# A wait for a gate transfer moved behind the first level's decays, and three weight casts moved behind the copies of v's second tile

## The chip, the core and the metric

The kernel runs on one core of one Trainium2 chip. A core has five engines with instruction streams of their own: PE (TensorE, matrix products; its weight loads are shown as PEld), DVE (VectorE), ACT (ScalarE), POOL (GpSimd) and SP, whose queue here issues nearly all DMA transfers. DVE, ACT, POOL and SP each work through their stream in the order in which the program lists it, so an instruction that waits holds up whatever stands behind it. The metric is the device time of one execution in microseconds (us), as the median of several runs.

## The reference

One inference step of one decoder layer over 1024 prompt tokens and eight short sample sequences of 8 tokens (1088 tokens together), in float32. One projection `w_in` (1024 x 7168) feeds two groups of recurrent heads; their outputs go through `w_out` and a residual.

```python
xn = rmsnorm(x, g_norm); proj = xn @ w_in            # xm zm om | fh qh ih zh
xc = silu(causal_conv(xm)); q, k = xc_h @ w_q, xc_h @ w_k; v = xm_h @ w_v
gates = concat(q, k, v) @ w_gate + b_gate             # ig, log_sigmoid -> lf
hm = mlstm_scan(q, k, v, ig, lf, C0, n0, m0)          # 4 heads, running-max stabiliser m
oh = hgrn2_scan(silu(qh), (1-lb)*sigmoid(-fh), ih, log(lb+(1-lb)*sigmoid(fh)), S0)   # 8 heads
y = x + concat(gated layernorm(hm), gated rmsnorm(oh)) @ w_out; y = rmsnorm(y, g_final)
```

The stabiliser `m` of the mLSTM heads is a running recurrence over the tokens, m_t = max(lf_t + m_(t-1), ig_t), started anew at each sample's first token from a given state.

## The kernel before, in words

**Exact float32 products.** Every large product is made of three passes: both operands are split into a high part and the remainder (`whi`, `wlo` for a block of weights, `XH`, `XL` for the tokens), and `mm3` issues high x high, low x high and high x low into one PSUM buffer (lines L94 to L96). A weight block of 128 output columns is loaded into `wraw`, cast to `whi` on ACT, and `wlo` is the difference, made on POOL or DVE (all three in `w_split`, line L147). `whi` and `wlo` have two buffers each, `wraw` three.

**The front.** `front_conv` makes two blocks of `xm` for each mLSTM head through `in_block`, whose token columns come in three chunks of 384, 384 and 320 (24 matmuls each). Each chunk lands in one of three PSUM buffers named `mm` and is emptied by ACT (L477 into `xmh`, L478 into `XB`) and DVE (L479 into `xml`). The third chunk also holds the samples' columns: L481 and L482 on ACT, L483 on DVE. `convolve` follows on DVE (L503, then L506 three times). `front_v` multiplies `xm` by `w_v` in nine tiles of 128 tokens, six matmuls each; each tile takes one of the three `mm` buffers and is emptied by two ACT copies, L540 (256 columns of v) and L541 (8 gate columns, into `GTOK` for head 0 and `GST` for the others). I number the tiles t0 to t8.

**Which block is split when.** In a call of `in_block` with one block, `blk_split(nxt)` splits the next block's weights ahead of the chunks. Blocks 5, 7 and 9 are split in the calls that follow `front_v` of heads 1, 2 and 3 in the program.

**The gate scans.** After the front, `gate_scan` writes the gates of all heads and tokens to memory (`gd`, L595), reads them back in rows of one head each (L597, four transfers: `glf`, `gt`, `ig`, `gy`), and runs two scans on DVE. In the scan of `m` the samples' first tokens are cut off by writing -1e30 into eight columns of `t1` (the tile `gt`), line L604. The scan itself is L606; `lm` (L603) is the start of the samples, and it had been put behind `ctxs["k2"]`, the copy of the first level's decays into `Sf` (L1038).

**The heads.** `hgrn_main` works a head in levels. For the first level DVE and ACT make `Q1`, `K1` (L1022, L1023, L987) from `hq` and `hk`, and PE then runs 72 small matmuls in a burst (L101). PE's order is written by `weave`, which slips the next blocks' `in_block` matmuls between the pieces of a head.

**What sets the order.** Up to the fourth `xm` block, the orders of PE, ACT, DVE and POOL are as written. Then a scheduler that works with a model of time places the instructions of all engines (from the heads on, PE's order is again as written), within the data's own order; `behind(i, r)` adds to it that `i` may not come before `r` on their engine.

Of the kernel before, what the change touches and what calls it, by code (L numbers as in the profile page):

```python
# [17 lines left out]
T = 1088  # L18
TP = 1024
# [11 lines left out]
def hybrid_step(  # L31
# [8 lines left out]
    V, S, G, PE = nc.vector, nc.scalar, nc.gpsimd, nc.tensor  # L40
# [28 lines left out]
    def ps_mm():  # L69
        return pm.tile([P, 512], F32, tag="mm", name=nm("mm"))  # L70
# [21 lines left out]
    def mm3(out, lhs, rhs, first, last):  # L92
        (lh, ll), (rh, rl) = lhs, rhs
        PE.matmul(out, lhsT=lh, rhs=rh, start=first, stop=False)  # L94
        PE.matmul(out, lhsT=lh, rhs=rl, start=False, stop=False)  # L95
        PE.matmul(out, lhsT=ll, rhs=rh, start=False, stop=last)  # L96
# [22 lines left out]
    r = 0  # L119
# [22 lines left out]
    def w_split(key, eng=G):  # L142
        raw = wq[key]
        hi = wp.tile([P, 1024], F32R, tag="whi", name=nm("whi"))
        lo = wp.tile([P, 1024], F32R, tag="wlo", name=nm("wlo"))
        wq[key] = (hi.rearrange("p (k c) -> p k c", c=P), lo.rearrange("p (k c) -> p k c", c=P))
        return S.copy(hi, raw), eng.tensor_tensor(lo, raw, f32(hi), op=ALU.subtract)  # L147
# [16 lines left out]
    def blk_load(i):  # L164
        if i < len(blocks) and ("w", i) not in wq:
            kind, j = blocks[i]
            o = boff[kind] + j * P
            return w_load(("w", i), w_in[0, :, o:o + P].rearrange("(k p) c -> p k c", p=P))

    def blk_split(i, eng=None):  # L170
        if i < len(blocks) and not isinstance(wq[("w", i)], tuple):
            return w_split(("w", i), eng or (V if i in v_splits else G))
# [34 lines left out]
    def xchunk(X, c):  # L207
        t0, n = CH[c]
        return X[:, 8 * t0:8 * t0 + 8 * n].rearrange("p (k c) -> p k c", c=n)
# [41 lines left out]
    def in_block(*items):  # L251


        ws = []
        for kind, j, evac in items:
            i = bidx[(kind, j)]
            if i > 1 or len(items) == 1:
                if ("w", i) in wq and not isinstance(wq[("w", i)], tuple):
                    blk_split(i)
            ws.append(i)  # L260
        for i in ws:
            blk_load(i + 2)
        nxt = ws[-1] + 1
        if len(items) == 1:
            blk_split(nxt)
        for c, (t0, n) in enumerate(CH):
            xh, xl = xchunk(XH, c), xchunk(XL, c)
            for (kind, j, evac), i in zip(items, ws):
                wh, wl = wq[("w", i)]
                ps = ps_mm()  # L270
                for k in range(8):
                    mm3(ps[:, :n], (wh[:, k, :], wl[:, k, :]), (xh[:, k, :], xl[:, k, :]), k == 0, k == 7)
                    if k % 2 and k < 7:
                        yield cost(6, n)
                evac(c, t0, n, ps)
                yield cost(6, n)
# [8 lines left out]
    ctxs = {}  # L285
# [93 lines left out]
    def behind(i, r):  # L379

        if r is None:
            return
        tc.add_manual_dep(getattr(i, "ins", i), getattr(r, "ins", r).name, mybir.DependencyInfo(
            mybir.DependencyClass.NoSync, mybir.DependencyReason.DATA), reason="behind")
# [42 lines left out]
    GTOK = cp.tile([P, 9, 8], F32, name="GTOK")  # L427
    GST = cp.tile([P, 9, 8], F32, name="GST")
# [96 lines left out]
    def front_v(h):  # L525
        wh, wl = qkv_w[h]
        xms = [fr[2 * h + a]["m"] for a in range(2)]
        for t in range(9):
            ps = ps_mm()
            u = t % 2  # L530
            if u == 0:
                vt = half("vt")
                vv = vt[:, :2 * VW].rearrange("p (a c) -> p a c", c=VW)
                G.memset(vv[:, :, 256:257], 1.0)
                G.memset(vv[:, :, 257:258], 0.0)
            for a in range(2):
                o = 512 + a * 264
                mm3(ps[:, :264], (xms[a][0][:, t * P:(t + 1) * P], xms[a][1][:, t * P:(t + 1) * P]),
                    (wh[:, o:o + 264], wl[:, o:o + 264]), a == 0, a == 1)
            S.copy(vv[:, u, 0:256], ps[:, :256])  # L540
            S.copy((GST if h else GTOK)[:, t, :], ps[:, 256:264])  # L541
            if t == 8:
                nc.sync.dma_start(out=vsd[h], in_=vt[:, :VW])
            elif u:
                nc.sync.dma_start(out=vd[h, :, (t - 1) * VW:(t + 1) * VW], in_=vt[:, :2 * VW])
            yield

        if h:
            V.tensor_tensor(GTOK, GTOK, GST, op=ALU.add)
# [33 lines left out]
    def gate_scan():  # L583

        ig, y, lf, t1, m, b = [unit(s)[0:4, :T] for s in ("ig", "gy", "glf", "gt", "gm", "gb")]

        lg = half("lg")
        LF = lg[:, 0:272]
        V.tensor_scalar(GT, GT, scalar1=bgt, scalar2=None, op0=ALU.add)
        S.activation(LF, GT, AF.Abs)  # L590
        S.activation(LF, LF, AF.Exp, scale=-1.0)
        S.activation(LF, LF, AF.Ln, bias=1.0)
        V.scalar_tensor_tensor(LF, GT, 0.0, LF, op0=ALU.min, op1=ALU.subtract)
        for i, src in enumerate((GT, LF)):
            nc.sync.dma_start(out=gd[i], in_=src)  # L595
        for i, dst in ((1, lf), (1, t1), (0, ig), (0, y)):
            nc.sync.dma_start(out=dst.rearrange("p (j t) -> p j t", t=272),  # L597
                              in_=gd[i].rearrange("(j r) t -> r j t", r=32)[4 * i:4 * i + 4])
        yield 1.0
        lfs = lf[:, TP:T].rearrange("p (b c) -> p b c", c=8)[:, :, 0]  # L600
        igs = ig[:, TP:T].rearrange("p (b c) -> p b c", c=8)[:, :, 0]
        lm = small(8, "lm")
        behind(V.tensor_tensor(lm[0:4, :], lfs, m0t, op=ALU.add), ctxs["k2"])  # L603
        V.memset(t1[:, TP:T].rearrange("p (b c) -> p b c", c=8)[:, :, 0], -1e30)  # L604
        V.tensor_tensor(y[:, TP:T].rearrange("p (b c) -> p b c", c=8)[:, :, 0], igs, lm[0:4, :], op=ALU.max)
        V.tensor_tensor_scan(m, t1, y, initial=0.0, op0=ALU.add, op1=ALU.max)  # L606
        yield 4.0
        G.memset(t1, 1.0)
        G.memset(t1[:, 0:TP].rearrange("p (b c) -> p b c", c=P)[:, :, 0], 0.0)
        G.memset(t1[:, TP:T].rearrange("p (b c) -> p b c", c=8)[:, :, 0], 0.0)  # L610
        st = lf[:, 0:TP].rearrange("p (b c) -> p b c", c=P)[:, 1:8, 0]
        V.tensor_tensor(st, st, m[:, 0:TP].rearrange("p (b c) -> p b c", c=P)[:, 0:7, 127], op=ALU.add)
        V.tensor_copy(lfs, lm[0:4, :])
        V.tensor_tensor_scan(b, t1, lf, initial=0.0, op0=ALU.mult, op1=ALU.add)
        V.tensor_tensor(y, b, m, op=ALU.subtract)
        nc.sync.dma_start(out=rd, in_=y)
        V.tensor_tensor(ig, ig, b, op=ALU.subtract)
        nc.sync.dma_start(out=o_pm[0, 0].unsqueeze(1), in_=m[:, TP - 1:TP])
        msl = small(8, "msl")
        V.tensor_copy(msl[0:4, :], m[:, TP:T].rearrange("p (b c) -> p b c", c=8)[:, :, 7])  # L620
        nc.sync.dma_start(out=o_sm[0].rearrange("b h -> h b"), in_=msl[0:4, :])
        yield 6.5
        ps = ps_o()
        for t in range(8):
            PE.transpose(ps[:, t * 8:t * 8 + 4], ig[:, t * P:t * P + P], ident[0:4, 0:4])
            PE.transpose(ps[:, t * 8 + 4:t * 8 + 8], m[:, t * P:t * P + P], ident[0:4, 0:4])
        for j in range(4):
            for o, src in ((64, ig), (68, m)):
                PE.matmul(ps[32 * j:32 * j + 32, o:o + 4], lhsT=src[:, TP + win(j):TP + win(j) + 32],
                          rhs=ident[0:4, 0:4], start=True, stop=True)  # L630
        V.tensor_copy(COLS.rearrange("p a b -> p (a b)"), ps[:, :72])
        S.activation(COLS[:, :, 4:8], COLS[:, :, 4:8], AF.Exp, scale=-2.0)
        yield 0.5

        co = unit("co")
        for kk in range(2):
            pt = ps_o()
            for k in range(4):
                PE.transpose(pt[:27, k * P:(k + 1) * P], CS[:, kk * 4 + k, :], ident)
            V.tensor_copy(co[:27, kk * 512:(kk + 1) * 512], pt[:27, :])  # L640
        nc.sync.dma_start(out=o_pconv[0, 0], in_=co[0:3, :DM])
        nc.sync.dma_start(out=o_sconv[0].rearrange("b j d -> (b j) d"), in_=co[3:27, :DM])
        yield 0.5
# [1078 lines left out]
```

## Time and profile before

| | |
|---|---|
| time, median of 3 runs | 1149.5 us (1148.18 to 1153.0) |
| time of the profiled execution | 1149.5 us |
| span of the profiled execution | 1147.7 us, so 1.8 us lie around it |
| mean granted TensorE clock | 0.995 |
| PE busy | 1123.9 us, 98% of the span |
| DVE, ACT, POOL busy | 749.7, 471.1, 239.7 us |
| DMA | 133.53 MB, mean 116 GB/s |

Times in the profile are in us from the span's start unless marked ns. A row of the timeline has start, duration, engine, line, operation, what is written and read, sizes, a count, and in brackets the idle time of the engine ahead of it and what ended it. A row of the waits has the engine, tile and line that waited, what it waited for, the total, the number of times and the longest. Matmuls overlap, so one of 0.33 us can start 0.17 us after another: the pace is read from the starts.

### The profile page before, as it was taken

Reading aid. Unit: us, or ns where it says so; the run is one execution under the profiler, and the core shown is the slowest. Engines: PE = TensorE matmul, PEld = TensorE weight load, DVE = VectorE, ACT = ScalarE, POOL = GpSimd, SP = SyncE. Lnnn points to the kernel's source line nnn. Section 1 sums busy time; section 2 is a strip of 40 time slices with the busy share of each in tenths; the row PEclk is TensorE's granted clock in tenths of the full one; section 3 lists DMA queues with packets and bytes.
Section 4 is the critical chain, followed back from the end, with each engine's and each line's share of the span. In section 5 each row is a group of like instructions: output and inputs, shape, how many; then the busy total and the mean of one; then the engine's idle time right before and its main releaser. Section 6 shows DMA issues by size and latency. Waiting matters only on the chain.

```text
span 1147.7 us, 22956 instructions
## 1 busy us (share of the span) xinstructions
PE 1123.9 (98%) x9255; PEld 1056.0 (92%) x9255; DVE 749.7 (65%) x1484; ACT 471.1 (41%) x1047; POOL 239.7 (21%) x396
## 2 busy tenths in 40 slices
PE   7989999899999999999999999999999999999997
PEld 6889999899999999999999999999999998888886
DVE  6656454494778567784779567877677687545533
ACT  6455455335432553235423453252524344243332
POOL 3204333002530144203530153102020200100000
PEclk9999999999999999999999999999999999999999
DMA  7243342222324242334124331422221255567662
GB/s 225 85 150 123 113 157 101 86 56 94 104 83 152 60 152 78 119 95 136 56 78 153 117 112 60 134 77 78 57 78 57 68 171 159 153 196 208 191 191 91
DMA packets 154154, 133.53 MB, mean 116 GB/s; under 512 B 11500, under 2 KB 130376, under 8 KB 154048
## 3 DMA queue, kind: packets, MB, share of 16 engines
q1 hardware_dynamic: 154046, 132.06, 36.9%
q8 instruction: 73, 1.20, 0.4%
q14 instruction: 33, 0.27, 0.1%
q10 hardware_dynamic: 2, 0.00, 0.0%
HBM read 93.47 MB, written 38.57 MB: 115 GB/s over the span
## 4 chain that ended last, share of the span: by engine, by line
PE 88%; DVE 5%; ACT 3%; DMA 2%; issue 2%; POOL 0%; SPq 0%; POOLq 0%; DVEq 0%; ACTq 0%
PE mm L94 24%; PE mm L95 23%; PE mm L96 23%; PE lv L101 2%; PE o L1216 1%; PE o L1235 1%; PE o L94 1%; PE o L95 1%; PE o L96 1%; PE o L1238 1%; DMA mraw<-mixd 1%; PE lv L1197 1%; PE o L1130 1%; PE mm L1338 1%; PE mm L1340 1%
## 5 line engine op out<-in xcount | busy, mean ns | idle before, releaser
L94 PE MATMUL mm<-XH,whi 128*128 128x384 f32 (+1 forms) x1344 | 450.4, 335 | 0.0
L95 PE MATMUL mm<-XL,whi 128*128 128x384 f32 (+1 forms) x1344 | 439.4, 327 | 0.4 <-DVE XL L245 0.4
L96 PE MATMUL mm<-XH,wlo 128*128 128x384 f32 (+1 forms) x1344 | 439.2, 327 | 0.0
L94 PEld LDWEIGHTS mm<-XH,whi 128*128 128x128 f32 x1344 | 253.5, 189 | 3.1 <-issue 2.5
L95 PEld LDWEIGHTS mm<-XL,whi 128*128 128x128 f32 x1344 | 253.5, 189 | 1.8 <-issue 0.9
L96 PEld LDWEIGHTS mm<-XH,wlo 128*128 128x128 f32 x1344 | 252.9, 188 | 0.0
L147 ACT CAST whi<-wraw 128x1024 fp32r<-128x1024 f32 x54 | 56.7, 1051 | 87.2 <-PE mm L95 67.2
L147 POOL TENSOR_TENSOR wlo<-wraw,whi 128x1024 fp32r<-128x1024 f32 x30 | 71.8, 2392 | 84.3 <-ACT whi L147 84.0
L1328 ACT CAST mhi<-mraw 128x1024 fp32r<-128x1024 f32 (+1 forms) x32 | 31.9, 998 | 69.3 <-PE mm L95 50.5
L974 POOL MEMSET A<- 128x288 f32 x8 | 2.7, 342 | 261.8 <-ACT A L1103 261.8
L94 PE MATMUL mm<-XH,mhi 128*128 128x512 f32 x144 | 56.8, 395 | 0.0
L96 PE MATMUL mm<-XH,mlo 128*128 128x512 f32 x144 | 56.3, 391 | 0.2 <-DVE mlo L1329 0.2
L95 PE MATMUL mm<-XL,mhi 128*128 128x512 f32 x144 | 56.1, 389 | 0.0
L1329 DVE TENSOR_TENSOR mlo<-mraw,mhi 128x1024 fp32r<-128x1024 f32 (+1 forms) x32 | 37.0, 1155 | 20.2 <-ACT mhi L1328 19.7
L922 DVE TENSOR_SCALAR f<-f,OML,LB 128x384 f32<-128x384 f32 (+1 forms) x24 | 32.9, 1369 | 10.7 <-ACT f L920 10.3
L479 DVE TENSOR_TENSOR xml<-mm,xmh 128x384 fp32r<-128x384 f32 (+1 forms) x24 | 12.3, 511 | 42.2 <-ACT XB L478 42.2
L96 PE MATMUL mm<-woh,mlo 128*128 128x512 f32 x96 | 37.5, 390 | 0.0
L147 DVE TENSOR_TENSOR wlo<-wraw,whi 128x1024 fp32r<-128x1024 f32 x24 | 29.3, 1220 | 12.5 <-ACT whi L147 12.5
L94 PE MATMUL mm<-woh,mhi 128*128 128x512 f32 x96 | 37.4, 389 | 0.0
L95 PE MATMUL mm<-wol,mhi 128*128 128x512 f32 x96 | 37.4, 389 | 0.0
L990 DVE TENSOR_TENSOR QK<-hk,Sf 128x256 f32<-128x256 f32 x96 | 36.1, 416 | 0.0
L1401 POOL TENSOR_TENSOR rs<-rs,mhalf 128x1 f32<-128x1 f32 (+1 forms) x9 | 4.9, 542 | 145.9 <-DVE rs L1400 145.9
(365 smaller groups left out, 2201.0 us busy)
## 6 DMA issues: line engine op xcount, KB each, us to landing
wraw<-in_w_in SPq DMA_DIRECT2D x56, 512.0 KB
woraw<-in_w_out SPq DMA_DIRECT2D x16, 512.0 KB
mraw<-mixd SPq DMA_DIRECT2D x16, 512.0 KB
mraw<-mixd SPq DMA_DIRECT2D x16, 448.0 KB
xcd<-XB SPq DMA_DIRECT2D x8, 544.0 KB
qkd<-qk SPq DMA_DIRECT2D x16, 272.0 KB
xcr<-xcd SPq DMA_DIRECT2D x8, 544.0 KB
mixd<-xcr SPq DMA_DIRECT2D x8, 544.0 KB
```

What stands on the lines that cost most here:

```text
L94: PE.matmul(out, lhsT=lh, rhs=rh, start=first, stop=False)
L95: PE.matmul(out, lhsT=lh, rhs=rl, start=False, stop=False)
L96: PE.matmul(out, lhsT=ll, rhs=rh, start=False, stop=last)
L101: i = PE.matmul(out, lhsT=lhsT, rhs=rhs, start=start, stop=stop)
L147: return S.copy(hi, raw), eng.tensor_tensor(lo, raw, f32(hi), op=ALU.subtract)
L479: evs.append(V.tensor_tensor(ml[:, t0:t0 + m], ps[:, :m], f32(mh[:, t0:t0 + m]), op=ALU.subtract))
L922: V.tensor_scalar(f[:, s], f[:, s], scalar1=OML[:, h:h + 1], scalar2=LB[:, h:h + 1], op0=ALU.mult, op1=ALU.add)
L990: i = V.tensor_tensor(dst, ksrc, ssrc, op=ALU.mult)
L1130: PE.transpose(pt[:, u * P:(u + 1) * P], iT[:, t * P:(t + 1) * P], ident)
L1197: PE.transpose(tp[:, u * P:(u + 1) * P], sq[:, u * P:(u + 1) * P], ident)
L1328: S.copy(hi[:, :w * n], raw[:, :w * n])
L1329: V.tensor_tensor(lo[:, :w * n], raw[:, :w * n], f32(hi[:, :w * n]), op=ALU.subtract)
```

## The change

Two edits. The clearing of the samples' places in `t1` gets the same ordering as `lm`: it may not come before the copy of the first level's decays. And `front_v` keeps the gate copy of its second tile (t1); the next single `in_block` puts the cast of the block that it splits behind that copy.

```diff
         if len(items) == 1:
-            blk_split(nxt)
+            r = blk_split(nxt)
+            if "v1" in ctxs:
+                behind(r[0], ctxs.pop("v1"))
...
             S.copy(vv[:, u, 0:256], ps[:, :256])
-            S.copy((GST if h else GTOK)[:, t, :], ps[:, 256:264])
+            gc = S.copy((GST if h else GTOK)[:, t, :], ps[:, 256:264])
+            if t == 1:
+                ctxs["v1"] = gc
...
         behind(V.tensor_tensor(lm[0:4, :], lfs, m0t, op=ALU.add), ctxs["k2"])
-        V.memset(t1[:, TP:T].rearrange("p (b c) -> p b c", c=8)[:, :, 0], -1e30)
+        behind(V.memset(t1[:, TP:T].rearrange("p (b c) -> p b c", c=8)[:, :, 0], -1e30), ctxs["k2"])
         V.tensor_tensor(y[:, TP:T].rearrange("p (b c) -> p b c", c=8)[:, :, 0], igs, lm[0:4, :], op=ALU.max)
```

Below the edits the line numbers shift by 2 in `front_v` and by 4 from `gate_scan` on: L481 before is L483 after, L604 before is L608 after. PE's order is the same row for row.

DVE where the first HGRN2 head begins; `gt` is `t1`, `wlo` the low part of block 10, `hq`, `Q`, `K`, `Sf` belong to the first head. Before:

```order
L930 TENSOR_TENSOR hq_2062<-hq_2062,mm_2285 128x384
L604 MEMSET gt_2342 4x8
L147 TENSOR_TENSOR wlo_2378<-wraw_2252,whi_2377 128x1024
L930 TENSOR_TENSOR hq_2062<-hq_2062,mm_2312 128x320
L1023 TENSOR_TENSOR Q_319_2364<-hq_2062,f_2060 128x544
L987 COPY K_320_2367<-hk_2061 128x256
L987 COPY K_320_2367<-hk_2061 128x4x64
L1038 COPY Sf_2363<-f_2060 128x544
L603 TENSOR_TENSOR lm_2459<-glf_2341,m0t 4x8
L1040 TENSOR_TENSOR f_2060<-f_2060 128x544
```

After:

```order
L934 TENSOR_TENSOR hq_2062<-hq_2062,mm_2285 128x384
L147 TENSOR_TENSOR wlo_2378<-wraw_2252,whi_2377 128x1024
L934 TENSOR_TENSOR hq_2062<-hq_2062,mm_2312 128x320
L1027 TENSOR_TENSOR Q_319_2364<-hq_2062,f_2060 128x544
L991 COPY K_320_2367<-hk_2061 128x256
L991 COPY K_320_2367<-hk_2061 128x4x64
L1042 COPY Sf_2363<-f_2060 128x544
L607 TENSOR_TENSOR lm_2459<-glf_2341,m0t 4x8
L608 MEMSET gt_2342 4x8
L1044 TENSOR_TENSOR f_2060<-f_2060 128x544
```

The memset went behind seven instructions, to the place after `lm`.

ACT where `xm`'s last chunk of block 3 (`mm_1012`) ends and head 1's `front_v` begins (`mm_1066` is t0, `mm_1078` t1, `mm_1088` t2); `whi_1184` is block 5. Before:

```order
L147 CAST whi_1184<-wraw_937 128x1024
L477 CAST xmh_935<-mm_1012 128x256
L478 COPY XB_933<-mm_1012 128x256
L540 COPY vt_1067<-mm_1066 128x256
L541 COPY GST<-mm_1066 128x8
L540 COPY vt_1067<-mm_1078 128x256
L541 COPY GST<-mm_1078 128x8
L481 COPY XB_933<-mm_1012 128x8x8
L482 CAST xmh_935<-mm_1012 128x128
L540 COPY vt_1089<-mm_1088 128x256
```

After:

```order
L479 CAST xmh_935<-mm_1012 128x256
L480 COPY XB_933<-mm_1012 128x256
L542 COPY vt_1067<-mm_1066 128x256
L543 COPY GST<-mm_1066 128x8
L483 COPY XB_933<-mm_1012 128x8x8
L484 CAST xmh_935<-mm_1012 128x128
L542 COPY vt_1067<-mm_1078 128x256
L543 COPY GST<-mm_1078 128x8
L147 CAST whi_1184<-wraw_937 128x1024
L542 COPY vt_1089<-mm_1088 128x256
```

The cast went from ahead of the last chunk's copies to behind t1's, and the samples' two copies came ahead of t1's. The same happens at heads 2 and 3 (blocks 7 and 9). On POOL the block's `wlo` goes behind two small copies (L500, L501), and on SP the load that takes over its `wraw` buffer goes behind two stores of v (L545).

PE has the same rows, but other waits, since the three PSUM buffers are given to the tiles of v otherwise. The first matmul of t4 (`mm_1110`) and of t5 (`mm_1122`), head 1, with the engines that each waits for. Before:

```order
L94 MATMUL mm_1110<-wqh_794,xmh_714 128x264 [waits PE_49,Activation_49]
L95 MATMUL mm_1110<-wql_795,xmh_714 128x264
L96 MATMUL mm_1110<-wqh_794,xml_715 128x264
L94 MATMUL mm_1122<-wqh_794,xmh_714 128x264 [waits DVE_49]
L95 MATMUL mm_1122<-wql_795,xmh_714 128x264
```

After:

```order
L94 MATMUL mm_1110<-wqh_794,xmh_714 128x264 [waits DVE_49]
L95 MATMUL mm_1110<-wql_795,xmh_714 128x264
L96 MATMUL mm_1110<-wqh_794,xml_715 128x264
L94 MATMUL mm_1122<-wqh_794,xmh_714 128x264 [waits PE_49,Activation_49]
L95 MATMUL mm_1122<-wql_795,xmh_714 128x264
```

The DVE instruction that is waited for is the last reader of the third chunk's buffer (L483 before, L485 after): t5 took that buffer, and now t4 takes it. The other wait is for the gate copy of t2 on ACT.

## The prediction

> **What bounds the kernel now.** I read the page's busy times first, then PE's own waits, then the timeline at each wait that the change touches.
>
> ```profile
> PE 1123.9 (98%) x9255; PEld 1056.0 (92%) x9255; DVE 749.7 (65%) x1484; ACT 471.1 (41%) x1047; POOL 239.7 (21%) x396
> ...
> PE lv L101 <- DVE K L987: 2.9, 1, 2.9
> ...
> PE mm L95 <- DVE xcl L522: 2.2, 1, 2.2
> PE mm L94 <- ACT GTOK L541: 1.6, 1, 1.6
> PE mm L94 <- ACT GST L541: 1.3, 3, 0.4
> ```
>
> PE is busy 98% of the span and does the same matmuls in the same order afterwards. So the change is worth what it takes out of, or puts into, PE's waits, and the pace right behind them. Two of these rows are its targets: the one wait of 2.9 us for `K` ahead of the first head's burst, and three of 0.4 us for `GST` copies, one in `front_v` of each of heads 1 to 3. The other engines' totals say nothing here.
>
> **The memset's stop.** DVE, ACT, SP and PE around it:
>
> ```profile
> 222.25 0.07 DVE L604 MEMSET gt<- 4x8 f32 x1 [5.05 <-DMA gt<-gd]
> 222.33 1.22 DVE L147 TENSOR_TENSOR wlo<-wraw,whi 128x1024 fp32r<-128x1024 f32 x1
> ...
> 224.62 0.49 DVE L987 COPY K<-hk 128x256 f32<-128x256 f32 x2
> ...
> 225.38 0.15 DVE L603 TENSOR_TENSOR lm<-glf,m0t 4x8 f32<-4x8 f32 x1
> ...
> 218.03 1.05 ACT L147 CAST whi<-wraw 128x1024 fp32r<-128x1024 f32 x1 [1.43 <-PE mm L95]
> ...
> 219.03 0.27 SPq L597 DMA_DIRECT2D glf<-gd  x1
> 219.39 0.25 SPq L597 DMA_DIRECT2D gt<-gd  x1
> ...
> 220.09 0.25 SPq L597 DMA_DIRECT2D gy<-gd  x1
> ...
> 222.00 0.34 PE L96 MATMUL mm<-XH,wlo 128*128 128x384 f32 x1
> 225.26 0.90 PE L101 MATMUL lv<-Q,K 128*32 128x64 f32 x32 [2.93 <-DVE K L987]
> ...
> 229.04 0.33 PE L95 MATMUL mm<-XL,whi 128*128 128x384 f32 x1
> ```
>
> A memset of 0.07 us holds DVE for 5.05 us, until `gt` has landed, 2.86 us after its issue (222.25 - 219.39). Behind it stand `wlo`, the last piece of `hq`, `Q` and `K`, and PE's burst waits for these. Without it `wlo` waits only for its cast, which ends at 218.03 + 1.05 = 219.08. I start it at 219.11, by the few hundredths that stand between an end and a follower elsewhere, so 3.22 us earlier. What stands between `wlo` and the burst is unchanged (2.93 us, 225.26 - 222.33), so the burst may start at 222.04.
>
> What PE makes of this is seen at the next head, where the same burst comes without a wait:
>
> ```profile
> 356.35 0.34 PE L96 MATMUL mm<-XH,wlo 128*128 128x384 f32 x1
> 356.62 0.65 PE L101 MATMUL lv<-Q,K 128*32 128x64 f32 x32
> ...
> 358.96 0.33 PE L95 MATMUL mm<-XL,whi 128*128 128x384 f32 x1
> ```
>
> There the burst starts 0.27 us after the last matmul ahead of it; here that would be 222.27, so the operands at 222.04 are there by 0.23 us. From that last matmul to the second matmul of the third group behind the burst it takes 358.96 - 356.35 = 2.61 us; here it took 229.04 - 222.00 = 7.04 us. The difference, **4.43 us**, is more than the wait, because PE runs slow for a while after it:
>
> ```profile
> 225.20:227.20 2.00, 1.94 (x82) 1.93 (x83) 2.00 (x6) 0.62 (x4) 0.00 (x0) 0.58 0.76 222
> 227.20:229.20 2.00, 2.00 (x8) 2.00 (x8) 2.00 (x2) 0.00 (x0) 0.39 (x1) 0.57 0.04 8
> 229.20:231.20 2.00, 2.00 (x14) 2.00 (x13) 2.00 (x8) 0.00 (x0) 1.74 (x6) 1.00 0.00 0
> ```
>
> (Stretch, its length, the busy time and count of PE, PEld, DVE, ACT and POOL, the granted clock, DMA share, GB/s.) The clock is 0.58 and 0.57 for the 4 us after the wait and 1.00 then. Of the 4.43 us, 225.26 - 222.27 = 2.99 are the wait and 1.44 the slow clock. [...]
>
> What is late next: `lm`, 3.22 us earlier at 222.16, needs `glf`, which with `gt`'s 2.86 us lands at 221.89. The memset behind it needs `gt` at 222.25 and may stop DVE for about 0.1 us; behind it stands L1040 (0.72 us), then the step that needs `gy`, landing at 222.95. These feed the scans and later levels, not the burst. If these reads came 1 us later, DVE would stop 1 us there, at a place from which PE's next burst is 20 us off:
>
> ```profile
> 246.57 1.19 PE L101 MATMUL lv<-QK 128*32 128x32 f32 x112
> ```
>
> If the cover of 0.23 us is gone, PE waits by what is missing. So the term's bounds are 0 (another operand takes the memset's place) and 4.43 us; I take 4.43, since each operand's time comes from rows.
>
> **The casts in the front.** All three places look alike; this is head 3's, with t0 from 178.09:
>
> ```profile
> 178.14 1.05 ACT L147 CAST whi<-wraw 128x1024 fp32r<-128x1024 f32 x1 [2.50 <-PE mm L95]
> 179.09 0.37 ACT L477 CAST xmh<-mm 128x256 fp32r<-128x256 f32 x1
> 179.36 0.38 ACT L478 COPY XB<-mm 128x256 f32<-128x256 f32 x1
> ...
> 179.88 0.19 ACT L541 COPY GST<-mm 128x8 f32<-128x8 f32 x1
> ...
> 180.26 0.28 ACT L481 COPY XB<-mm 128x64 f32<-128x64 f32 x1
> ...
> 181.15 0.37 ACT L540 COPY vt<-mm 128x256 f32<-128x256 f32 x1 [0.45 <-PE mm L96]
> ...
> 179.76 0.42 DVE L479 TENSOR_TENSOR xml<-mm,xmh 128x256 fp32r<-128x256 f32 x1 [3.54 <-ACT XB L478]
> 180.64 1.61 DVE L503 TENSOR_SCALAR Y<-XB,PAR 128x1112 f32<-128x1112 f32 x1 [0.46 <-ACT XB L481]
> 182.18 0.28 DVE L483 TENSOR_TENSOR xml<-mm,xmh 128x128 fp32r<-128x128 f32 x1
> ...
> 178.09 0.28 PE L94 MATMUL mm<-wqh,xmh 128*128 128x264 f32 x1
> ...
> 178.70 0.28 PE L96 MATMUL mm<-wqh,xml 128*128 128x264 f32 x1
> ...
> 180.12 0.39 PE L94 MATMUL mm<-wqh,xmh 128*128 128x264 f32 x1 [0.42 <-ACT GST L541]
> ...
> 180.83 0.28 PE L96 MATMUL mm<-wqh,xml 128*128 128x264 f32 x1
> ...
> 181.68 0.35 PE L94 MATMUL mm<-wqh,xmh 128*128 128x264 f32 x1
> ...
> 182.51 0.39 PE L94 MATMUL mm<-wqh,xmh 128*128 128x264 f32 x1
> ...
> 183.35 0.28 PE L94 MATMUL mm<-wqh,xmh 128*128 128x264 f32 x1
> ```
>
> The PE rows are t0's first and last matmul, t2's first and last, and the first of t4, t5 and t6, read by their starts. From t0's two rows, five steps take 0.61 us, so a tile takes 0.73 us and t2 would start at 179.55 without a wait; it starts at 180.12. The cast delays the copies of the last chunk and of t0, and t2 wants t0's buffer.
>
> After the change ACT begins that chunk 0.32 us after its last matmul (the lag between 180.83 and 181.15), and this matmul of 320 columns stands some 0.15 us ahead of t0 (264 columns take 0.122): 177.94 + 0.32 = 178.26, 0.83 us earlier than 179.09. t0's copy starts at 178.70 + 0.32 = 179.02, its gate copy 0.26 us later at 179.28, and t2 0.24 us after that (180.12 - 179.88) at 179.52: no wait. But t4 now takes the third chunk's buffer, which L483 releases. L481 follows L479, which follows L478, so L503 and L483 move with the chunk by 0.83 us, and with the 0.33 us between 182.18 and 182.51 the buffer is free at 182.51 - 0.83 = 181.68. **t4 starts at 181.68, exactly as before.** The gap of 0.57 us at t2 becomes one of 0.67 us at t4 (pace: 178.09 + 4 x 0.73 = 181.01). The cast now runs about 180.1 to 181.15, and t5's buffer, that of t2, is copied behind it and free near 181.55, before t5 wants it at 182.5. Only the second small stop, at t5 (its 0.84 us to t6 against 0.73 us), goes: 0.1 us a place, **0.3 us** in all.
>
> The bounds: if t4 finds its buffer free, the place takes 9 x 0.73 = 6.6 us where it took 7.45 us (to the end of t8 at 183.35 + 3 x 0.73 = 185.54), a gain of 0.86 us, 2.6 us over three. If L503 and L483 stay where they are in time, t4 starts at 182.51, 0.83 us late, and three places lose 2.2 us with the 0.3 us still gained. I take 0.3, since the rows say what L503 waits for.
>
> What else moves costs nothing: block 9's `wlo` on POOL moves with its cast by 2 us (178.14 to 180.1), and PE needs that block only behind a whole block of 72 matmuls that starts at 185.5; the load that takes over the buffer starts 2 us later, and its cast is for a later block still; the two stores that pass it on SP issue as their tiles are copied, and no load waits for them.
>
> **Sum.** 4.43 + 0.3 = 4.7 us from a profiled execution of 1149.5 us (span 1147.7 and 1.8 around it), which is also the median of the runs: 1144.8 us, 0.41% less.
>
> **The rivals.**
>
> *The gaps in the front vanish too.* For it: the cast was the cause of all three, and the samples' copies come earlier. Against it: L503's 1.61 us stand ahead of L483. 1149.5 - 4.4 - 2.6 = 1142.5 us.
>
> *The slow clock stays.* [...] As a mechanism here: the slow 4 us come at their own time and only the 2.99 us go. Against it: they begin with the first matmul behind the wait. 1149.5 - 3.0 - 0.3 = 1146.2 us.
>
> *The gain is not there, or is given back.* The burst finds `K` as late as before because another transfer or operand stops DVE ahead of it, or PE waits later instead. For it: DVE is busy from 222 us on without a break and comes only 3.2 us earlier while PE comes 4.4 earlier. Against it: the burst's operands are all traced above, and PE's next bursts have room. About 1149 us.
>
> *Slower: t4's wait grows until it halves the clock.* A wait of 1.6 us (`GTOK`, above) and one of 2.2 us are in the trace, and only the longer is followed by a slow clock:
>
> ```profile
> 76.00:80.00 4.00, 3.82 (x21) 3.52 (x21) 1.74 (x4) 1.51 (x6) 0.28 (x3) 0.66 0.48 144
> ```
>
> If L483 came 1.5 us later than I put it, for instance with one of the L506 ahead of it too, t4 would wait 2.2 us. Then each place takes 6.6 + 2.2 + 1.4 (34% of 4 us) = 10.2 us in place of 7.45: three lose 8.2 us, and with 4.4 gained the time is 1153.3 us. That decides from a wait between 1.6 and 2.2 us on. Against it: the order of DVE has L503 alone ahead of L483.
>
> **Chances.** The forecast 0.60, with its own range 1143.3 to 1146.3, since the runs before lie 1.3 below and 3.5 above their median; the gaps vanish 0.14; the clock stays 0.11; no gain 0.10; slower 0.05. A change of 0.5%, 5.75 us, is about what a measurement of this kernel can tell from none; the forecast lies 1 us short of it. I give 0.3 of the forecast's 0.60 to the far side (0.18) and nearly all of the second case (0.14): faster 0.32. Slower by more than 0.5% would be over 1155.2 us, past even the slow rival: 0.03. The rest, 0.65, is the same. The range 1142.0 to 1148.2 holds the forecast, the vanishing gaps and the slow clock, and leaves out most of no gain and all of slower.
>
> **What would show it.** DVE's wait for `gt` is gone or under 0.3 us, and stands behind `Sf`; PE's wait of 2.9 us for `K` is gone; the granted clock is 1.00 in the 8 us from the burst on. In the front PE's three waits are for L485 (DVE), 0.5 to 0.7 us, no longer for `GST`, and each stretch from t0 to the end of t8 takes 7.3 to 7.4 us. The prediction is wrong if PE still waits over 0.5 us at the first burst, if the clock still falls there, or if the three stretches take under 7.0 us or over 7.6.

## The result, and the profile after

| | before | after |
|---|---|---|
| time, median of 5 runs each | 1149.5 us (1148.18 to 1153.0) | 1143.95 us (1142.97 to 1145.23) |
| span of the profiled execution | 1147.7 us | 1142.2 us |
| mean granted TensorE clock | 0.995 | 0.996 |

The ratio of the times is **0.9947** (95% interval 0.9929 to 0.9965), 0.53% less; the interval holds the 0.5% that the prediction took as the least that can be told from none. The medians lie 5.5 us apart. Run twice more beside the experiments below, the changed kernel stood to the kernel before at 0.9932 (0.9915 to 0.9949) and 0.9940 (0.9919 to 0.9961). The forecast was 1144.8 us.

The page's busy times of the changed kernel, and three rows of PE's waits:

```profile
PE 1122.0 (98%) x9255; PEld 1055.2 (92%) x9255; DVE 753.9 (66%) x1484; ACT 471.2 (41%) x1047; POOL 240.9 (21%) x396
```

```profile
PE mm L95 <- DVE xcl L524: 2.2, 1, 2.2
PE mm L94 <- ACT GTOK L543: 1.6, 1, 1.6
...
PE mm L94 <- DVE xml L485: 0.2, 1, 0.2
```

Both targets are gone: no row for `K`, none for `GST`. The waits of 2.2 and 1.6 us, near 73 and 52 us, stand as before. The one wait for L485 of 0.2 us is not at one of the three places. But DVE is busy 4.2 us longer than before (753.9 against 749.7) with the same 1484 instructions. That is a first sign that something else changed.

**The memset's place.** DVE and PE around the first burst, after:

```profile
217.84 1.22 DVE L147 TENSOR_TENSOR wlo<-wraw,whi 128x1024 fp32r<-128x1024 f32 x1 [1.97 <-ACT whi L147]
...
220.15 0.49 DVE L991 COPY K<-hk 128x256 f32<-128x256 f32 x2
...
221.01 0.07 DVE L608 MEMSET gt<- 4x8 f32 x1
...
220.68 0.34 PE L96 MATMUL mm<-XH,wlo 128*128 128x384 f32 x1
220.95 0.65 PE L101 MATMUL lv<-Q,K 128*32 128x64 f32 x32
...
223.30 0.33 PE L95 MATMUL mm<-XL,whi 128*128 128x384 f32 x1
```

`wlo` waits for its cast and nothing else, the memset finds `gt` landed, and the burst follows the last matmul by 0.27 us. From that matmul to the second matmul of the third group behind the burst PE takes 2.62 us (220.68 to 223.30); it took 7.04. The windows show no slow clock (the last three numbers of a row are the clock, the DMA share and GB/s):

```profile
221.00:223.00 2.00, 2.00 (x87) 1.97 (x87) 2.00 (x6) 0.61 (x3) 0.00 (x0) 1.00 0.73 193
223.00:225.00 2.00, 2.00 (x13) 2.00 (x12) 2.00 (x3) 0.00 (x0) 0.64 (x1) 1.00 0.04 8
```

**The front.** ACT, DVE, POOL and PE at head 3's place, after; the PE rows are the first matmuls of t0, t2 and t4, and the first of the block that follows:

```profile
177.79 0.37 ACT L479 CAST xmh<-mm 128x256 fp32r<-128x256 f32 x1 [2.65 <-PE mm L96]
...
179.57 1.07 ACT L147 CAST whi<-wraw 128x1024 fp32r<-128x1024 f32 x1
...
179.25 0.86 DVE L505 TENSOR_SCALAR Y<-XB,PAR 128x1112 f32<-128x1112 f32 x1 [0.36 <-ACT XB L483]
180.02 0.28 DVE L485 TENSOR_TENSOR xml<-mm,xmh 128x128 fp32r<-128x128 f32 x1
180.22 4.81 DVE L508 SCALAR_TENSOR_TENSOR Y<-XB,PAR,Y 128x1112 f32<-128x1112 f32 x2
...
180.72 3.14 POOL L147 TENSOR_TENSOR wlo<-wraw,whi 128x1024 fp32r<-128x1024 f32 x1 [1.31 <-ACT whi L147]
...
177.59 0.28 PE L94 MATMUL mm<-wqh,xmh 128*128 128x264 f32 x1
...
179.05 0.35 PE L94 MATMUL mm<-wqh,xmh 128*128 128x264 f32 x1
...
180.57 0.28 PE L94 MATMUL mm<-wqh,xmh 128*128 128x264 f32 x1
...
184.22 0.34 PE L94 MATMUL mm<-XH,whi 128*128 128x384 f32 x1
```

From t0 to the block behind t8 it is 6.63 us (177.59 to 184.22), where it was 7.44; the other two places took 6.63 too (before 7.45 and 7.44). So the three give 2.44 us, eight times the 0.3 us of the forecast. t4 does not wait, and the reason is in the first DVE row: the conv's first product, the same instruction on the same shapes, takes 0.86 us where it took 1.61. What stood beside it before was POOL's `wlo`; these are two POOL rows of the kernel before, and the grouping of all eight products there and here (ns, least, median and most):

```profile
179.27 2.39 POOL L147 TENSOR_TENSOR wlo<-wraw,whi 128x1024 fp32r<-128x1024 f32 x1 [6.85 <-ACT whi L147]
181.58 0.72 POOL L500 COPY front<-XB 128x3 f32<-128x3 f32 x1
...
L503 DVE TENSOR_SCALAR Y<-XB,PAR x8: 851/1502/2949, 50.8 to 180.6; 128x1112 f32<-128x1112 f32 x8
```

```profile
L505 DVE TENSOR_SCALAR Y<-XB,PAR x8: 850/858/2950, 50.5 to 179.2; 128x1112 f32<-128x1112 f32 x8
```

Of the 1.61 us (180.64 to 182.25), 0.86 would be work from 181.39 on, which is 0.27 us before the record of `wlo` ends at 181.66. After the change `wlo` comes later and meets the L508s instead, two of which take 4.81 us together, and `wlo` itself takes 3.14 us in place of 2.39. The groups of the two pages, before and after (busy time, mean ns of one):

```profile
L506 DVE SCALAR_TENSOR_TENSOR Y<-XB,PAR,Y 128x1112 f32<-128x1112 f32 x24 | 32.9, 1371 | 0.4
```

```profile
L508 DVE SCALAR_TENSOR_TENSOR Y<-XB,PAR,Y 128x1112 f32<-128x1112 f32 x24 | 39.0, 1626 | 0.4
```

That is 6.1 us more, and three products are 2.25 us shorter (3 x 0.75): 3.9 of DVE's 4.2 us. PE has no new wait for it.

**What was given back.** t0 of head 1 starts at 98.38 us, at 97.25 before, though nothing that was changed lies ahead of it. The windows around PE's wait for `xcl`, before:

```profile
71.91:75.32 3.41, 0.69 (x4) 0.26 (x2) 1.76 (x3) 3.20 (x7) 0.15 (x1) 1.00 0.41 163
75.32:78.73 3.41, 3.18 (x12) 2.89 (x13) 2.42 (x5) 1.08 (x4) 0.32 (x4) 0.50 0.24 70
```

and after:

```profile
71.29:74.70 3.41, 1.05 (x7) 0.62 (x5) 1.49 (x3) 3.29 (x7) 0.00 (x0) 1.00 0.41 163
74.70:78.11 3.41, 2.81 (x11) 2.52 (x12) 2.79 (x6) 1.23 (x5) 0.47 (x4) 0.50 0.16 45
78.11:81.53 3.42, 3.42 (x17) 3.42 (x17) 0.00 (x0) 0.79 (x2) 0.00 (x0) 0.50 0.62 190
```

The half clock lasted 3.4 us in the one execution and 6.8 in the other. From the end of the wait for `xcl` to the first L101 behind it PE took 7.50 us before (75.37 to 82.87) and 8.87 after (75.11 to 83.98), 1.37 us more; 0.26 of them are made up by the wait ending that much earlier. So the two spans differ by -4.42 (memset) - 2.44 (front) + 1.13 (ahead of head 1) + 0.2 (the rest of the program) = -5.5 us.

### The profile page after: what moved, and what is told of

Read it like the earlier page. It is cut to its first block, busy times and chain, and to the rows that moved or that the text cites. A ratio compares the mean times of both kernels' runs of the same rounds, so it can differ in the third digit from the quotient of the medians.

```text
span 1142.2 us, 22958 instructions
## 1 busy us (share of the span) xinstructions
PE 1122.0 (98%) x9255; PEld 1055.2 (92%) x9255; DVE 753.9 (66%) x1484; ACT 471.2 (41%) x1047; POOL 240.9 (21%) x396
## 4 chain that ended last, share of the span: by engine, by line
PE 88%; DVE 5%; DMA 3%; ACT 2%; issue 1%; POOL 0%; SPq 0%; POOLq 0%; ACTq 0%; DVEq 0%
PE mm L94 24%; PE mm L95 24%; PE mm L96 24%; PE lv L101 2%; PE o L1220 1%; PE o L94 1%; PE o L96 1%; PE o L95 1%; PE o L1239 1%; DMA RB<-rd 1%; PE o L1242 1%; DMA mraw<-mixd 1%; PE lv L1201 1%; PE o L1134 1%; PE mm L1342 1%
## 5 line engine op out<-in xcount | busy, mean ns | idle before, releaser
L508 DVE SCALAR_TENSOR_TENSOR Y<-XB,PAR,Y 128x1112 f32<-128x1112 f32 x24 | 39.0, 1626 | 0.4
L481 DVE TENSOR_TENSOR xml<-mm,xmh 128x384 fp32r<-128x384 f32 (+1 forms) x24 | 12.3, 512 | 37.4 <-ACT XB L480 37.4
```

Source lines behind the costliest of these rows:

```text
L481: evs.append(V.tensor_tensor(ml[:, t0:t0 + m], ps[:, :m], f32(mh[:, t0:t0 + m]), op=ALU.subtract))
L508: V.scalar_tensor_tensor(Y[:, :1112], XB[:, j:j + 1112], cw[:, 8 * j + ft:8 * j + ft + 1], Y[:, :1112], op0=ALU.mult, op1=ALU.add)
```

## The experiments

**One edit at a time.** First the memset's move alone:

```diff
-        V.memset(t1[:, TP:T].rearrange("p (b c) -> p b c", c=8)[:, :, 0], -1e30)
+        behind(V.memset(t1[:, TP:T].rearrange("p (b c) -> p b c", c=8)[:, :, 0], -1e30), ctxs["k2"])
```

> The kernel before with the memset's move alone. Theory (the two edits act at different places and add up): the last matmul ahead of the first burst to the second matmul of the third group behind it takes 2.6 us in place of 7.0, the granted clock is 1.00 from the burst on, and the three places in front_v keep their 7.45 us each, with three waits for GST copies. Median 4.4 us under before: 1145.1. Rival (the front casts made the gain, the memset's was paid back later): 1148 to 1149.5 with the wait for K gone all the same.

1146.48 us against 1150.04 us of the kernel before beside it, ratio 0.9967 (0.9952 to 0.9983): 3.6 us less, where 4.4 were forecast. In the trace the burst's stretch is 2.61 us (first and last row below), the places are 7.45, 7.43 and 7.44 us, and the clock is 1.00 from the burst on:

```profile
223.95 0.34 PE L96 MATMUL mm<-XH,wlo 128*128 128x384 f32 x1
...
226.56 0.33 PE L95 MATMUL mm<-XL,whi 128*128 128x384 f32 x1
```

Then the front casts' move alone:

```diff
-        behind(V.memset(t1[:, TP:T].rearrange("p (b c) -> p b c", c=8)[:, :, 0], -1e30), ctxs["k2"])
+        V.memset(t1[:, TP:T].rearrange("p (b c) -> p b c", c=8)[:, :, 0], -1e30)
```

> The changed kernel with the memset back in its old place, so the front casts' move alone. Theory (the three places give 0.82 us each and nothing takes it back): places of 6.63 us, the wait of 2.9 us for K and the slow clock behind it as before, median 2.4 us under before: 1147.1. Rival A (what the changed kernel lost ahead of the first place, 1.1 us at t0 of head 1, comes with this edit): 1148.4 and t0 of head 1 again at 98.4. Rival B (the prediction's own: t4 takes over the wait): places of 7.35 us, 1149.2.

1147.52 us, ratio 0.9974 (0.9962 to 0.9986): 2.5 us less, and three places of 6.63 us. So the front casts are worth what the places show, and the prediction's own 0.3 us falls. The two parts add up: 3.6 + 2.5 = 6.1 us, where the changed kernel's three ratios give 6.1, 7.8 and 6.9 us. Rival A's sign did come, t0 of head 1 at 98.20 us; but with the memset alone, which lacks this edit, it came at 99.22, so the later start does not need this edit, and the time is nearer to the theory's 1147.1 than to the rival's 1148.4.

What I had not expected is at the burst. The transfer of `gt` took as long as before, 2.88 us from issue to the memset, but PE was later: `gt` was there 0.52 us ahead of PE's last matmul (219.98 against 220.50), where it had come 0.25 us behind it (222.25 against 222.00). The same stop looks so in the waits and the windows:

```profile
PE lv L101 <- DVE K L991: 2.2, 1, 2.2
```

```profile
217.96:221.37 3.41, 2.88 (x17) 2.55 (x15) 1.38 (x3) 0.00 (x1) 0.00 (x0) 1.00 0.06 16
221.37:224.79 3.42, 1.79 (x84) 1.80 (x85) 3.39 (x10) 1.83 (x6) 0.00 (x0) 1.00 0.51 153
```

A stop of 2.16 us, and no slow clock behind it, though a stop as long near 73 us (2.2 us for `xcl`) halves the clock in the same execution, for 6.83 us from 74.60 on. The price of the memset's stop is thus not one number. By the stretch from the last matmul to the second of the third group it was 7.04 - 2.61 = 4.43 us in the profile of before. Here it is 4.81 - 2.61 = 2.20 us:

```profile
220.50 0.34 PE L96 MATMUL mm<-XH,wlo 128*128 128x384 f32 x1
...
225.31 0.33 PE L95 MATMUL mm<-XL,whi 128*128 128x384 f32 x1
```

In the profile of the kernel with the casts left in place (below), PE waits 3.20 us and the half clock lasts until 233.53 us, past the third group, so I measure to PE's next burst, first there and then in the changed kernel:

```profile
223.91 0.34 PE L96 MATMUL mm<-XH,wlo 128*128 128x384 f32 x1
227.45 1.08 PE L101 MATMUL lv<-Q,K 128*32 128x64 f32 x32 [3.20 <-DVE K L991]
...
249.96 1.19 PE L101 MATMUL lv<-QK 128*32 128x32 f32 x112
```

```profile
240.83 1.19 PE L101 MATMUL lv<-QK 128*32 128x32 f32 x112
```

From the last matmul ahead of the stop that is 26.05 us against 20.15 (240.83 - 220.68) without a stop, so 5.9 us. By the same measure the stop of before cost 4.42 us (246.57 - 222.00 = 24.57).

**Does POOL beside DVE lengthen the product?** Four POOL subtractions more, put behind the conv-state copies:

```diff
-        G.tensor_copy(CS[:, ft, 3:27].rearrange("p (b c) -> p b c", c=3), sv[:, :, 8:11])
+        cs = G.tensor_copy(CS[:, ft, 3:27].rearrange("p (b c) -> p b c", c=3), sv[:, :, 8:11])
+        if ft in (3, 5, 7):
+            for _ in range(4):
+                cs2 = G.tensor_tensor(junk, CF[:, 0:256], CF[:, 0:256], op=ALU.subtract)
+                behind(cs2, cs)
+                cs = cs2
```

> The changed kernel with four GpSimd subtractions of 128x256 more, into a tile that nobody reads, behind the samples' copies of the conv's blocks 3, 5 and 7, so that GpSimd works on two inputs while VectorE makes the conv's first product in front_v; nothing is left out. Theory (VectorE and GpSimd slow each other when both run, and GpSimd's wlo beside it made that product 1.61 us long in the kernel before): the product takes 1.3 to 1.6 us again, t4 waits 0.3 to 0.7 us for VectorE's second xml, the three places take 7.0 to 7.35 us, and the time is 1 to 2 us over the changed kernel: 1145 to 1146. Rival (ACT's cast ahead of the copies was the whole cause, and the product's length depends on something else than GpSimd): the product stays at 0.86 us, places at 6.63, 1144.

1143.93 us, ratio 0.9949 (0.9931 to 0.9968), places of 6.63 us: the theory's numbers did not come. DVE and POOL at head 3:

```profile
177.92 0.86 DVE L511 TENSOR_SCALAR Y<-XB,PAR 128x1112 f32<-128x1112 f32 x1 [0.36 <-ACT XB L484]
...
178.90 6.60 DVE L514 SCALAR_TENSOR_TENSOR Y<-XB,PAR,Y 128x1112 f32<-128x1112 f32 x3
...
178.04 2.86 POOL L507 TENSOR_TENSOR junk<-CF 128x256 f32<-128x256 f32 x2
```

The product is untouched. It had begun 0.12 us before the first subtraction, and it is the subtractions that are long: 1.43 us each for 256 columns, where 512 columns take 1.04 us if POOL is first (the subtraction in "POOL first" below). So the two engines do not seem to slow each other evenly, and the theory had to become a sharper one: **the one that begins first keeps the other out.** The rival foresaw the same 0.86 us, so this run alone does not rule it out.

**The casts where they were, `wlo` elsewhere.** Now POOL's work beside the product goes (these three `wlo` are made on DVE, behind `cv`) and ACT's cast stays ahead of the copies:

```diff
-            blk_split(nxt)
+            r = blk_split(nxt, V if nxt in (5, 7, 9) else None)
+            if nxt in (5, 7, 9) and r is not None:
+                behind(r[1], ctxs.pop("cv"))
...
+            if j == 1 and ft in (3, 5, 7):
+                ctxs["cv"] = cv
```

(`cv` is the conv's first L506 of the block.)

> The kernel before with ACT's casts where they were, but the wlo of the conv's three front blocks made on VectorE behind its second product instead of on GpSimd, so that nothing of GpSimd's weight split runs beside the conv's first product. Theory (GpSimd's wlo lengthens the product, ACT's cast delays t2): the product takes 0.86 us in place of 1.61, the wait of 0.4 us for the GST copy ahead of t2 stays, the small second stop at t5 goes, and the places take 7.2 to 7.35 us; the wait for K stays at 2.9 us; time within 1 us of before: 1148.5 to 1149.5. Rival (the product's length comes from ACT reading the same tile or from its own operands): it keeps 1.61 us.

1150.46 us, ratio 0.9997 (0.9982 to 1.0012), places of 7.36, 7.32 and 7.32 us, where the theory had 7.2 to 7.35. Head 3's product, and PE's wait there:

```profile
182.69 0.86 DVE L505 TENSOR_SCALAR Y<-XB,PAR 128x1112 f32<-128x1112 f32 x1 [0.45 <-ACT XB L483]
```

```profile
PE mm L94 <- ACT GST L545: 1.3, 3, 0.4
```

Without `wlo` beside it the product takes 0.86 us; t2 waits for its `GST` copy all the same. So the place has two causes one behind the other: ACT's cast, which held t2 for 0.57 us, and POOL's `wlo`, which would have held t4 for 0.67 us once t2 ran. The change removes both with one move, since `wlo` follows its cast. Taking `wlo` away alone gave 0.1 us a place (this run). Taking the cast away with `wlo` still beside the product is what I had forecast the change to be, at the same 0.1 us; no run has just that, and the nearest is the longer subtraction below, with places of 7.54 to 7.67 us.

**POOL first.** One subtraction, behind the first copy of conv state instead of the second, so that it is under way when DVE comes:

```diff
-        G.tensor_copy(CS[:, ft, 0:3], XB[:, 1024:1027])
+        cs = G.tensor_copy(CS[:, ft, 0:3], XB[:, 1024:1027])
+        if ft in (3, 5, 7):
+            behind(G.tensor_tensor(junk, junk, junk, op=ALU.subtract), cs)
```

> The changed kernel with one GpSimd subtraction of 128x512, on a tile that nobody else reads, behind the first of the two copies of conv state (L502) of blocks 3, 5 and 7, so that it is running when VectorE comes to the conv's first product; nothing is left out. Theory (whichever of the two engines begins first keeps the other out until its instruction is through; so the product's 1.61 us of the kernel before were 0.75 us of standing still for GpSimd's wlo, and 0.86 of work): the subtraction takes about 1.2 us from 0.2 us behind L502 on, the product comes out at 1.3 to 1.6 us, VectorE's second xml and with it t4's buffer 0.5 to 0.7 us later, and as the buffer was free 0.2 us early, t4 waits 0.2 to 0.5 us: places of 6.9 to 7.15 us in place of 6.63, time 1 to 1.5 us over the changed kernel. Rival (GpSimd's work beside VectorE's product costs the product nothing; ACT's cast was the whole cause): the product stays at 0.86 us and the places at 6.63.

1143.83 us, ratio 0.9934 (0.9913 to 0.9954). The subtraction was shorter than I had put it, and so the effect:

```profile
98.39 1.03 POOL L506 TENSOR_TENSOR junk<-junk 128x512 f32<-128x512 f32 x1
...
98.87 1.15 DVE L509 TENSOR_SCALAR Y<-XB,PAR 128x1112 f32<-128x1112 f32 x1 [0.36 <-ACT XB L485]
```

The product came out at 1.15, 1.04 and 1.02 us and the places at 6.81, 6.69 and 6.69: longer, not by the numbers expected, and too little to see in the time. The length follows the rule: 99.42 - 0.26 = 99.16 is when POOL lets go, 0.29 us after the product's start, and 0.86 + 0.29 = 1.15. The 0.26 us are not fitted to this row: with 0.86 us of work, all five products beside `wlo` from 99 us on in the profile of before begin it 0.25 to 0.27 us ahead of the end of `wlo`'s record. The one of 2.95 us near 84 us begins it 0.19 us ahead. To make it plain I doubled the elements, in half the bytes each:

```diff
-    junk = cp.tile([P, 512], F32, name="junk")
+    junk = cp.tile([P, 1024], mybir.dt.bfloat16, name="junk")
```

> As the kernel with one GpSimd subtraction of 128x512 f32 behind L502, with a subtraction of 128x1024 bf16 in its place; nothing is left out. Theory (VectorE's product stands still until 0.26 us before the record of GpSimd's instruction ends, then takes its 0.86 us): if twice the elements take twice the 1.04 us, the subtraction runs from 177.7 to 179.8 on that kernel's clock, the product comes out at 0.86 + (179.8 - 0.26 - 178.33) = 2.0 to 2.1 us, t4 waits, and the places take 6.63 + 1.2 - 0.1 = 7.6 to 7.8 us; 3 times 1.1 = 3.3 us over the changed kernel, 1147. If the bf16 elements go two at a time, the subtraction and the product look as in that kernel. Rival (the lengthening has another cause than GpSimd's instruction being under way): 1.0 to 1.15 us and 6.7 to 6.8 again although the subtraction is longer. On the slow clock behind PE's stop near 73 us, from ten profiles: the half clock lasts 3.41 us if PE idles at most 0.25 us in the first 3.41 us of it, and 6.83 us if it idles 0.35 us or more; and if it comes at all, PE idled over 2.0 us in the 3.41 us ahead of its begin.

1146.64 us, where the changed kernel beside it took 1144.39 (ratios to before 0.9970, 0.9957 to 0.9982, and 0.9940): 2.25 us more, where 3.3 were expected. Head 3:

```profile
179.54 1.89 POOL L506 TENSOR_TENSOR junk<-junk 128x1024 bf16<-128x1024 bf16 x1
...
180.15 1.88 DVE L509 TENSOR_SCALAR Y<-XB,PAR 128x1112 f32<-128x1112 f32 x1 [0.36 <-ACT XB L485]
...
182.29 0.39 PE L94 MATMUL mm<-wqh,xmh 128*128 128x264 f32 x1 [0.65 <-DVE xml L487]
```

POOL lets go at 179.54 + 1.89 - 0.26 = 181.17; with 0.86 us the product would end at 182.03, and it does (180.15 + 1.88). t4 waits 0.65 us for L487 (L485 of the changed kernel), and the places take 7.67, 7.54 and 7.54 us. This is the wait at t4 that the prediction described, made on purpose: the way from the product over L485 to t4 was right, and only the length of the product was not.

> The changed kernel a third time, beside the one with the longer subtraction: 1143 to 1145 us, product 0.86 us, places 6.63 us. For the slow clock behind PE's stop near 73 us the same rule: 3.41 us with at most 0.25 us of idle PE in its first 3.41 us, 6.83 us with 0.35 or more, and over 2.0 us of idle in the 3.41 us ahead of it.

The changed kernel beside it: 1144.39 us, places of 6.64, 6.63 and 6.64 us, half clock for 6.84 us with 1.11 us of idle PE in its first 3.41 us.

**The slow clock at 75 us.** If PE's stop for `xcl` sets it off, a shorter stop should remove it. In the part of the program that is written by hand, `xcl` goes ahead of the next block's chunk on DVE, and the casts of head 1's q/k weights behind that block:

```diff
         next(c1)
-        run(islice(third, 4))
         run(c1)
-        next(prep)
+        run(islice(third, 4))
         run(islice(third, 4))
         run(third)
+        next(prep)
```

> The changed kernel with the second block's xcl (VectorE) ahead of the next front block's chunk and the casts of head 1's q/k weights behind that block's last chunk, in the part of the program that is written by hand. Theory (PE's wait of 2.2 us for xcl near 73 us sets off the half clock behind it, which lasted 3.3 us in one profile and about 6.4 in five): the wait shrinks to 0.9 us, the granted clock stays at 1.00 from 74 to 83 us, t0 of head 1 comes at 94 to 96 us, and the time is 2.5 to 4.5 us under the changed kernel: 1139.5 to 1141.5. Rival (the half clock there comes at its own time, whatever the wait): the clock still falls between 74 and 83 us and only the 1.3 us of the wait go: 1142.7.

1141.29 us, ratio 0.9909 (0.9892 to 0.9927), and t0 of head 1 at 96.31 us; the changed kernel beside it:

> The changed kernel once more, beside the three others on the same chip: 1143 to 1145 us, spans from t0 to the next block of 6.63 us at the three places, and, by the theory that PE's stop of 2.2 us near 73 us sets off a slow clock of varying length, the half clock from 75 us on for 3.3 or 6.4 us.

1144.05 us, and half clock for 6.84 us. With the shorter stop:

```profile
PE mm L95 <- DVE xcl L524: 0.9, 1, 0.9
```

```profile
75.00:76.00 1.00, 0.62 (x3) 0.45 (x4) 1.00 (x3) 0.31 (x2) 0.19 (x1) 1.00 0.05 17
76.00:77.00 1.00, 0.88 (x6) 0.68 (x7) 0.42 (x2) 0.84 (x4) 0.28 (x3) 1.00 0.00 0
77.00:78.00 1.00, 0.99 (x7) 0.85 (x7) 0.90 (x2) 1.00 (x4) 0.00 (x0) 1.00 0.02 8
```

The clock is 1.00 all through, and 2.8 us are gone between the medians, more than the 1.3 us by which the wait shrank. The two intervals against the kernel before overlap, but the slowest run here (1142.24) is under the fastest of the changed kernel beside it (1142.51). That speaks for the stop and against a slow clock that comes at its own time, as far as one edit shows that moves two things. One more step of this kind, for the wait of 1.6 us near 52 us:

```diff
-        next(c0)
         run(islice(first, 4))
         run(first)
         next(c0)
+        next(c0)
```

> The kernel c1_ahead with the first block's conv step (VectorE: L505 and one L508, 2.2 us) behind the second block's last two chunks instead of ahead of them. Theory: the wait of 1.6 us for the GTOK copy near 52 us, which no slow clock follows, shrinks to 0.3 us or goes, and the time falls by 1.0 to 1.6 us more: 1138.5 to 1140.5. Rival (the conv's 2.2 us come late for PE instead, since VectorE is the busier engine there): the wait near 73 us grows by as much, and the time is that of c1_ahead or over it.

**1139.40 us**, ratio 0.9896 (0.9878 to 0.9914), the fastest here and 4.65 us under the changed kernel beside it. The row for `GTOK` is gone from the waits, and `xcl` still waits 0.9 us, so nothing was pushed on. By the intervals alone it is not told apart from the one before.

## Why the prediction was right, and where not

**The memset's term: right.** 4.43 us were forecast and 4.42 came in the profiled execution, each step at its place: `wlo` waits for its cast, `K` is ready at 220.64 and PE comes to the burst after it, the memset finds its data, the clock is 1.00. What I took for a constant was a sample, though: the 1.44 us of slow clock in it changed from execution to execution, with none, 3.4 or 6.8 us of half clock behind the same stop (below), and the stop itself on when `gt` lands. The 3.6 us by which the medians differ with the memset alone lie between the 2.20 and 5.9 us that the stop cost in single traces.

**The front's term: wrong, 0.3 us for 2.44.** The prediction said that it is wrong if the three stretches take under 7.0 us, and they take 6.63. The step that failed is "L503's 1.61 us stand ahead of L483". That L503 would begin as much earlier as its chunk was right: from t0 it is 1.66 us now (179.25 - 177.59) and was 2.55 (180.64 - 178.09), 0.89 earlier against a forecast of 0.83. But I moved its start and kept its length, when 0.75 us of that were POOL's `wlo`, which the same change moves away. A row in the trace of before said so: the product's least time was 851 ns. I also costed `wlo`'s move at nothing since PE needs it late, which holds, and did not ask what runs beside its old and its new time. The upper bound that I had kept for this term, 2.6 us, was the right end of it, and the first rival, at a chance of 0.14, is what happened in the front, though it named the cast as the one cause and not `wlo`.

The traces agree with DVE and POOL taking turns by whole instructions to within 0.27 us: counted back by its 0.86 us from its end, the product begins its work 0.27 us before `wlo`'s record ends (181.39 against 181.66), and 0.26 before the subtractions' ends in the two kernels with POOL first (99.16 against 99.42, 181.17 against 181.43). Had I read the overlapping rows of DVE and POOL so, I would have put the product at 0.86 us and t4's buffer free at 181.68 - 0.75 = 180.93 us, ahead of t4's pace of 181.01, and the term at its upper bound of 2.6 us, an estimate from the trace of before alone.

**The sum: near for two reasons that cancel, so in part by luck.** 4.43 + 2.44 would be 1142.6 us, the first rival's 1142.5. The runs lie 1.3 us above that, and in the traces t0 of head 1 comes 1.13 us later: 1.37 us from the slow clock at 75 us, less 0.26 us of an earlier start. That slow clock was 3.4 us long in the profile of before from which I worked, and 6.8 in all three of the changed kernel. It is not shown to belong to the change: the memset alone and the casts alone had 6.8 us too, and the two kernels with POOL first, which hold both edits, had 3.4.

**The other rivals.** The slow clock behind the burst went with the stop. No transfer took the memset's place. t4's wait did not arise at all, so the slower case fell with it; made by hand at 0.65 to 0.77 us, such a wait cost 0.9 to 1.0 us a place, and the only fall of the clock in that profile is the one at `xcl`.

## What to carry to other kernels

When a change moves an instruction of DVE or POOL, look at what ran beside it on the other of the two, before and after: a row that is longer than the least of its group may hold a wait, and that wait moves when its neighbour does. Price a stop of PE by several executions, or by a range, since the slow clock behind it came in steps of nothing, 3.4 or 6.8 us for nearly the same stop. And a place with two causes one behind the other shows only the first one in the waits; the forecast for removing it is the second one's wait, with that one's own reason looked up too.

## What the runs showed of the hardware that I had not expected

**The half clock came in whole stretches of 3.41 us, whole multiples of that length apart.** In the profile of before it begins at 75.32 and at 225.52 us (read from the clock of windows of 1 us) and lasts 3.41 us each time, to 78.73 and 228.93; in that of the changed kernel it lasts 6.83 us, from 74.70 to 81.53. The two of before begin 150.20 us apart, 44 steps of 3.414 us. In that of the casts left in place it is 226.70 - 76.52 = 150.18 us, 44 steps of 3.413; in the second execution of the changed kernel 76.76 - 18.74 = 58.02 us, 17 steps of 3.413. This grid lay differently against the stop for `xcl` from one execution to the other: the clock fell 0.05 us ahead of the end of PE's wait before (75.32 against 75.37) and 0.41 us ahead of it after the change (74.70 against 75.11). Nor was PE idle for a whole stretch ahead of a fall: it was busy for 0.5 to 1.25 us of the 3.41 us ahead of each fall in the table. This is what the rows show at the stops for `K` and `xcl` (idle is the window's length less PE's busy time):

| execution, stop | idle PE in the 3.41 us before | idle in the first 3.41 us of half clock | half clock |
|---|---|---|---|
| before, `K` | 2.93 | 0.00 | 3.4 us |
| before, `xcl` | 2.72 | 0.23 | 3.4 us |
| POOL first (512), `xcl` | 2.74 | 0.22 | 3.4 us |
| POOL first (1024), `xcl` | 2.79 | 0.21 | 3.4 us |
| after, `xcl` | 2.36 | 0.60 | 6.8 us |
| memset alone, `xcl` | 2.50 | 0.60 | 6.8 us |
| casts alone, `xcl` | 2.46 | 0.50 | 6.8 us |
| POOL beside, `xcl` | 2.20 | 0.75 | 6.8 us |
| casts left in place, `xcl` | 2.20 | 0.83 | 6.8 us |
| casts left in place, `K` | 2.46 | 0.74 | 6.8 us |
| after, second and third run, `xcl` | 2.16, 2.16 | 0.92, 1.11 | 6.8 us |
| casts alone, `K` | 0.53 and 1.63 | | none |

At these two stops, one that the grid cuts in two, like the last row's (its stretches are counted on from that execution's fall at 74.60 us), lowered nothing; one that filled 2.16 us or more of a stretch lowered the clock at its end, and where PE idled 0.5 us or more in the next stretch, two went slow. Two of the rows (POOL first with 1024, after's third run) are of executions that came after I had put this down, and they fit it.

But PE's idle time is not what decides. In three executions, the second and third of the changed kernel and the one with the casts left in place, the clock also fell for 3.4 us near 19 us, and PE had idled only 1.36, 1.70 and 1.40 us of the stretch ahead; the last row's 1.63 us lowered nothing. The second execution of the changed kernel:

```profile
15.32:18.73 3.41, 2.05 (x11) 1.28 (x10) 3.41 (x5) 2.79 (x5) 2.65 (x3) 1.00 1.05 345
18.73:22.15 3.42, 3.42 (x15) 3.42 (x14) 2.71 (x4) 2.22 (x4) 1.54 (x5) 0.50 1.17 194
```

The idle time of the weight loads (PEld) divides the cases. In the ten profiles of the table it was 2.09 to 3.17 us in the 15 stretches ahead of a fall, and at most 1.92 us in every other stretch at full clock between 15 and 1125 us. That is read from the rows afterwards: where between 1.92 and 2.09 us the limit lies is open, and I moved no stop against the grid on purpose.

**DVE and POOL took turns by whole instructions**, for a product with one tensor input (0.86 to 1.61 or 1.88 us). For the products with two inputs, L506 before and L508 after, the length fits it and no run tests it: head 3's three took 4.18 us together before, 1.39 each, and 6.22 us with `wlo` beside them. If the second of those begins its 1.39 us 0.26 us before `wlo`'s record ends (180.72 + 3.14 = 183.86), it ends at 184.99; the record of the first two ends at 180.22 + 4.81 = 185.03.
